# Interleaving the two parts of the up weights and shifting a row buffer by 64 bytes in a one-core decoder layer

## The chip, the cores and the metric

The kernel runs on one core of a Trainium2 chip. The core has a matrix engine (TensorE, in profiles PE, with its weight loads shown apart as PEld), a vector engine (VectorE, DVE), a scalar engine (ScalarE, ACT), a general engine (GpSimd, POOL) and a queue engine (SyncE, SP) that issues most transfers. The on-chip memory is laid out as 128 partitions; a tile has the same byte offset in all of them, and in this text an address is that offset. The metric is the time of one execution on the device in microseconds, and the kernel before takes 1039.2 us as the median of three runs (1038.97 to 1039.4).

## What is computed

One decoder layer on a sequence of 1024 rows of 1024 float32 values. A token mixer with two head groups comes first, then a gated MLP with a causal convolution of three taps:

```python
h = rms_norm(x, mix_norm)
z = h @ w_in                          # 1024 x 2320, columns for both head groups
# group A: chunked gated linear attention; group B: sliding-window attention with sinks
x = x + concat([o_gla, o_swa]) @ w_out
h2 = rms_norm(x, ffn_norm)
u = causal_dwconv(h2 @ w_up, conv_w, conv_b)      # 1024 x 5632
a, b = split(u, 2)
x = x + (silu(a) * b) @ w_down                    # 2816 -> 1024
```

The products with `w_up` (1024 x 5632) and `w_down` (2816 x 1024) are the larger part of the work.

## The kernel before, in words

**Precision.** A large product is made of float32 values that are split in two parts, a high one in the rounded type `float32r` and a low one, what is left of the value. Three matmuls replace one: high by high, high by low, low by high (`PASSES`). The function `split` makes the parts: ScalarE casts the high part into a tile (line 97), and GpSimd, or VectorE where a call says so, subtracts it from the source and writes the low part (line 100).

**Activations.** `big` holds the normalized and transposed rows of all eight row tiles, eight blocks of 128 features deep, high and low: `big[p, half, k, part, tile, column]`. `rows(t, ks, r)` is the piece of one row tile. In the first half of the program the pieces of `big` are the weights of matmuls (`dense`, line 327), and the projections' weights are the moving operand. In the MLP `big` is the moving operand: four row tiles, 512 columns, lie side by side.

**Up products.** The up projection of each block of 128 columns is done by a scheme of Strassen's kind: seven products (`P1` to `P7`) of 12 matmuls in place of eight. Each multiplies a weight operand (`A11`, `A12`, `A22` or a sum or difference `S1` to `S4`) by an activation operand. `B11`, `B21`, `B22` and `T1` lie in `big`; the sums `T2`, `T3` and `T4` lie in a second buffer, `ex`, which `norm2_sums` writes. So four of the seven products read `big` and three read `ex`. A weight operand is 4 blocks of 128 x 128, high and low, in a slot of 4096 bytes; `up_operand` (lines 782 to 808) makes it two products ahead, and `product` (line 843 issues the matmuls) uses it as the stationary side. There are 22 column blocks of each half (`a` and `b` of the MLP side by side), so 22 x 7 x 12 = 1848 up matmuls; those of the first block write banks named `gb` in the profile, all others `fb`.

**Down products.** After the third block, units of 6 down matmuls (`down_pair`, line 1024, written to `dn_P`) are put between the up products. Their operands lie in slots 4 to 7 and are written high part first, low part behind it, each in one run. VectorE adds each result to the rows `acc` (line 1028). The last two blocks go by `last_row` (line 1053).

**Order.** The order of the work is written by hand: each step gets a due time (`at`, `at_us`), the steps are sorted by it, and every engine runs its instructions in that order.

**Edges.** The convolution needs the last two values of the 512 rows before. `save_edge` (line 901) copies them out of the bank into a tile of two values; two such tiles take turns. They come from the pool `ff`, which is opened late.

**Addresses.** Pools on the left side stack upwards in the order in which they are opened: the base pool, then `acc`, then `ex`, then the pool of the second normalization, in whose place `ff` is opened afterwards. The weight slots lie on the right side. In the built program of before, `big` starts at 1152, `ex` at 112448, and the slots at addresses such as 204672. The remainder by 256 is 128 for `big` and for the slots, and 64 for `ex` and for two operands of the second block (`A11`, `A12`), which lie in the normalization's pool.

Some matmuls of the mixer are plain float32 and count twice in the profile: the scores of the linear attention (`ga`, line 601) are of this kind. The matmuls `dec` (line 548) have two columns only.

Of the kernel before, what the change touches and what calls it, by code (L numbers as in the profile page):

```python
# [9 lines left out]
F32 = mybir.dt.float32  # L10
F32R = mybir.dt.float32r
# [6 lines left out]
P = 128  # L18
T = 1024
D = 1024  # L20
NT = T // P
KD = D // P
# [12 lines left out]
def hymba_layer_kernel(ctx, tc, x, mix_norm, w_in, w_alpha2, b_alpha, gla_norm,  # L35
# [3 lines left out]
    act, dve, pool, pe, sp = nc.scalar, nc.vector, nc.gpsimd, nc.tensor, nc.sync  # L39
# [10 lines left out]
    base = ctx.enter_context(tc.tile_pool(name="base", bufs=1))  # L50
# [4 lines left out]
    def bank(name):  # L55
        ps["n"] += 1
        if "f" in ps:
            return ps["f"][2 + ps["n"] % 2]

        for start, which in (("n2pt_6", "b"), ("do1_7", "a"), ("n2pt_3", "a")):  # L60
            if name.startswith(start):
                return ps[which].tile([P, 512], F32, tag="b", name=name)
        return ps["ab"[ps["n"] % 2]].tile([P, 512], F32, tag="b", name=name)

    big = base.tile([P, 2, KD, 2, 4, P], F32R, name="big")

    def rows(t, ks, r):
        return big[:, t // 4, ks, r, t % 4, :]

    RAW_BUFS, K4, K2, N_WARM = 3, 6, 5, 5  # L70

# [13 lines left out]
    def slot_tile(slot, name, dt=F32R):  # L85
        return w_keep.tile([P, 2, 512], dt, tag=f"w{slot}", name=name, bufs=1)
# [8 lines left out]
    def split(src, hi, lo, eng=None, hi_eng=None):  # L95
        if hi_eng is None:
            act.copy(hi, src)  # L97
        else:
            hi_eng.tensor_copy(hi, src)
        (eng or pool).tensor_sub(lo, src, hi.bitcast(F32))  # L100
# [89 lines left out]
    def norm1_tr(t, i):  # L190
        tr_hi(t, i, xts["h", t], "n1")

    def norm1_lo(t, i):
        tr_lo(t, i, "n1")
# [32 lines left out]
    def norm2_sums(t):  # L227

        i, ex, pn = t - 4, fin["ex"], fin["pn"]
        p0, p1 = fin["pb", t]  # L230

        def put(src, hi, lo):
            split(src, hi, lo, dve)

        def extra(n):
            return ex[:, n, :, 0, i, :], ex[:, n, :, 1, i, :]

        def own(ks):
            return rows(t, ks, 0), rows(t, ks, 1)

        b12 = pn.tile([P, 4, P], F32, tag="b12", name=f"b12_{t}", bufs=1)
        b11, b21 = ([rows(i, ks, r).bitcast(F32) for r in range(2)] for ks in (slice(0, 4), slice(4, 8)))
        act.copy(b12, p0)
        put(p1, *own(slice(4, 8)))
        dve.tensor_sub(p0, p0, b11[0])
        dve.tensor_sub(p0, p0, b11[1])
        put(p0, *own(slice(0, 4)))
        dve.tensor_sub(p1, p1, b12)
        put(p1, *extra(1))
        dve.tensor_add(p1, p1, b11[0])  # L250
        dve.tensor_add(p1, p1, b11[1])
        put(p1, *extra(0))
        dve.tensor_sub(p0, b21[0], p1)
        dve.tensor_add(p0, p0, b21[1])
        put(p0, *extra(2))

    trs = {}

    def tr_hi(t, q, h, tag):
        pt = bank(f"{tag}pt_{t}_{q}")  # L260
        for k in range(4):
            c = (q * 4 + k) * P
            pe.transpose(pt[:, k * P:(k + 1) * P], h[:, c:c + P], ident)
        trs[tag, t, q] = pt.rearrange("p (k c) -> p k c", k=4)
        act.copy(rows(t, slice(q * 4, q * 4 + 4), 0), trs[tag, t, q])

    def tr_lo(t, q, tag):
        hi, lo = (rows(t, slice(q * 4, q * 4 + 4), r) for r in range(2))
        dve.tensor_sub(lo, trs[tag, t, q], hi.bitcast(F32))

    def norm_tr(t, h, tag):
# [5 lines left out]
    blocks = {}  # L277
# [45 lines left out]
    def dense(t, ws, n, name):  # L323
        pb = bank(name)
        for k in range(KD):
            for i, (ra, rb) in enumerate(PASSES):
                pe.matmul(pb[:, :n], lhsT=rows(t, k, ra), rhs=ws[k][:, rb, :n],  # L327
                          start=(k == 0 and i == 0), stop=(k == KD - 1 and i == 2))
        return pb

# [299 lines left out]
    def gate_tr(t, gs):  # L630
        pb = bank(f"ogt{t}")
        for h in range(4):
            pe.transpose(pb[:, h * P:(h + 1) * P], gs[:, h * P:(h + 1) * P], ident)
        pv = pb.rearrange("p (h c) -> p h c", h=4)
        hi, lo = (rows(t, slice(0, 4), r) for r in range(2))
        act.activation(hi, pv, AF.Copy, scale=glan)
        dve.scalar_tensor_tensor(lo, pv, glan, hi.bitcast(F32), op0=ALU.mult, op1=ALU.subtract)
        src = qo[:, t, :].rearrange("p (j c) -> p j c", j=4)
        hi, lo = (rows(t, slice(4, 8), r) for r in range(2))
        split(src, hi, lo)  # L640


    fin = {}
# [19 lines left out]
    def open_norm2():  # L663
        st.close()
        w_late["pool"] = swp.enter_context(tc.tile_pool(name="wb", bufs=1, side="right"))
        xp = ctx.enter_context(tc.tile_pool(name="xp", bufs=1))
        fin["ex"] = xp.tile([P, 3, 4, 2, 4, P], F32R, name="ex")
        fin["sn"] = ExitStack()
        pn = fin["pn"] = fin["sn"].enter_context(tc.tile_pool(name="pn", bufs=1))
        ffn = fin["ffn"] = pn.tile([P, D], F32, name="ffn")  # L670
        sp.dma_start(ffn, ffn_norm.partition_broadcast(P).rearrange("p o d -> p (o d)"))
        fin["s1"] = pn.tile([P, 4, P], F32, name="s1_0")
# [18 lines left out]
    psb = {}  # L691
# [18 lines left out]
    def unit_q_part(t, k0, k1):  # L710
        if k0 == 0:
            psb["q", t] = bank(f"dq{t}")
        pb = psb["q", t]
        for k in range(k0, k1):

            for i, (ra, rb) in enumerate(((0, 0), (1, 0), (0, 1))):
                pe.matmul(pb, lhsT=rows(t, k, ra), rhs=blocks["q"][k][:, rb, :],  # L717
                          start=(k == 0 and i == 0), stop=(k == KD - 1 and i == 2))

    def q_done(t):  # L720
# [56 lines left out]
    def sums(s1, a11, a21, a22, eng=pool):  # L777
        eng.tensor_add(s1, a21, a22)
        eng.tensor_sub(a21, a11, a21)
        eng.tensor_sub(a11, s1, a11)  # L780
# [7 lines left out]
    def up_operand(ch, name):  # L788
        ra, rb = raws["u", ch, 0], raws.get(("u", ch, 1), raws["u", ch, 0])
        a11, a12, a21, a22 = ra[:, 0:4], ra[:, 4:8], rb[:, 0:4], rb[:, 4:8]  # L790
        src = {"A11": a11, "A12": a12, "A21": a21, "A22": a22, "S2": a11, "S3": a21,
               "S4": a11 if ch else a12}.get(name)
        if name == "S2" and ch:
            s1 = psb["S1", ch] = fin["ff"].tile([P, 4, P], F32, tag="s", name=f"S1_{ch}", bufs=1)
            sums(s1, a11, a21, a22)
        elif name == "S1":
            src = psb["S1", ch]
        elif name == "S4" and ch:
            pool.tensor_sub(a11, a12, a11)
        slot = U_SLOT.get((ch, name))  # L800
        if slot is None:
            slot = 1 + -turn[0] % 3
            turn[0] += 1
            U_SLOT[ch, name] = slot
        w = fin["pn"].tile([P, 2, 512], F32R, name=f"{name}w_{ch}") if slot < 0 else slot_tile(slot, f"{name}w_{ch}")
        w = w.rearrange("p r (k n) -> p r k n", k=4)
        split(src, w[:, 0], w[:, 1], dve if ch < 2 and name[1] == "1" and name[0] == "A" else None)
        blocks["u", ch, name] = w

    def b_operand(name, k, r):  # L810
        ex = fin["ex"]
        return {"B11": big[:, 0, k, r], "B21": big[:, 0, 4 + k, r],
                "B22": big[:, 1, 4 + k, r], "T1": big[:, 1, k, r],
                "T2": ex[:, 0, k, r], "T3": ex[:, 1, k, r], "T4": ex[:, 2, k, r]}[name]

    PROD = {"P1": ("A11", "B11"), "P2": ("A12", "B21"), "P3": ("S4", "B22"), "P4": ("A22", "T4"),
            "P5": ("S1", "T1"), "P6": ("S2", "T2"), "P7": ("S3", "T3")}
# [77 lines left out]
        act.copy(dst, pb)  # L895

    def save_edge(ch, key, pb):
        e = psb[key, ch] = fin["ff"].tile([P, 2], F32, tag="e", name=f"{key}_{ch}", bufs=2)
        act.copy(e, pb[:, 510:512])

    def c11(ch):
# [196 lines left out]
    for c in halves:  # L1098
        split(mix_row[:, c], mix_hl[0][0:1, c], mix_hl[1][0:1, c], dve)
        pb = bank(f"mix{len(mix_ps)}")  # L1100
# [77 lines left out]
    for t in range(NT):  # L1178
        s = 11.0 + 1.9 * t
        at(s - (0.7 if t == 4 else 0.3), swa_qt, t)  # L1180
        at(s + 1.0, swa_scores, t, 0)
        at(s + 1.6, swa_scores, t, 1)
        at(s + 3.2, swa_pt, t, 0)
        at(s + 3.8, swa_pt, t, 1)
        at(s + 4.9, swa_pv, t)
        s = TG + t
        at(s - 2.4, gla_lh, t)
        at(s - 1.4, gla_exp, t)
        at(s + 1.0, gla_tr, t)
        if t < NT - 1:  # L1190
            if t:
                at(s + 1.75, gla_mid, t + 1)
            at(s + 1.8, gla_state, t)
        at(s + 1.9, gla_a, t)
        at(s + 2.7, gla_o, t)
        at(TR + t + 1.3, lambda tt=t: gate_tr(tt, psb.pop(("r", tt))))
# [23 lines left out]
    for ch, i, name in order:  # L1220
# [7 lines left out]
        if ch < 2 or (ch, i) == (2, 0):  # L1228
            n = 0
        elif ch < L - 1 or (ch, i) == (L - 1, 0):  # L1230
            n = 1
        else:
            n = 2
# [24 lines left out]
    for p in range(NPAIR):  # L1258
        for k in range(7):

            n = 7 * p + k - 2
# [51 lines left out]
```

## Time and profile before

| | |
|---|---|
| median of three runs | 1039.2 us |
| profiled execution | 1039.1 us, span 1037.4 us |
| TensorE busy | 1030.0 us (99%), 4976 matmuls |
| weight loads busy | 849.3 us (82%) |
| VectorE / ScalarE / GpSimd busy | 793.4 / 480.6 / 618.4 us |
| granted clock of TensorE | full throughout |
| idle time of TensorE before up products (`fb`) | 0.0 us |

The profile shows one execution. A group of instructions is given by line, engine, operation, output and inputs, shape and count; then follow the busy time of the group in us (overlaps counted once), the mean duration of one in ns, and the idle time of the engine before them with what ended it. Matmuls overlap: the next one starts before the last has ended, so a mean duration is longer than the distance from one to the next. That distance is read from the timeline, where equal neighbours are merged into one row with start, length and count.

### The profile page before, as it was taken

To read this page: it belongs to the slowest core of one execution; us is meant where nothing else is said; L and a number is where in the kernel's file an instruction comes from. 1 tells how busy PE (TensorE), PEld (TensorE's weight loads), DVE (VectorE), ACT (ScalarE), POOL (GpSimd) and SP (SyncE) were. 2 spreads that over 40 slices of the span, in tenths; PEclk is the share of its full clock that TensorE was granted. 3 is DMA by queue.
4 is the path that set the end of the run, shared out by engine and by line. 5 is a ranking of instruction groups with operands and counts; after the bars stand their busy time and mean duration, and the time that the engine had idled before them with its cause. 6 is when DMAs were issued, how large, how long until landed. Compare 5 with 4: busy or idle time off the path is not lost.

```text
span 1037.4 us, 13921 instructions
## 1 busy us (share of the span) xinstructions
PE 1030.0 (99%) x4976; PEld 849.3 (82%) x4976; DVE 793.4 (76%) x1332; ACT 480.6 (46%) x988; POOL 618.4 (60%) x510
## 2 busy tenths in 40 slices
PE   9999999999999999999999999999999999999998
PEld 6899887888888888888888888888888888888887
DVE  6776667755131699887979899897979798998976
ACT  5627655445340446554444445444444444454441
POOL 4592132325550205867868787877778787978750
PEclk9999999999999999999999999999999999999999
DMA  6152113002044202112120111222121211121104
GB/s 217 61 154 62 45 50 93 21 1 82 1 122 163 61 1 82 41 41 82 41 81 26 57 45 57 61 62 62 41 82 41 62 41 47 55 62 61 41 21 162
DMA packets 67502, 67.13 MB, mean 65 GB/s; under 512 B 4648, under 2 KB 52201, under 8 KB 67434
## 3 DMA queue, kind: packets, MB, share of 16 engines
q1 hardware_dynamic: 63448, 61.27, 18.9%
q10 hardware_dynamic: 3986, 4.99, 2.0%
q8 instruction: 39, 0.64, 0.2%
q14 instruction: 29, 0.24, 0.1%
HBM read 57.33 MB, written 4.19 MB: 59 GB/s over the span
## 4 chain that ended last, share of the span: by engine, by line
PE 97%; DMA 1%; DVE 1%; ACT 0%; issue 0%; POOL 0%; DVEq 0%; ACTq 0%; SPq 0%
PE fb L843 39%; PE dn_P L1024 18%; PE do L327 8%; PE dr L327 4%; PE dg L327 4%; PE dv L327 4%; PE dq L327 3%; PE dk L327 2%; PE gb L843 2%; PE dq L717 1%; PE pv L500 1%; PE fb L1053 1%; PE dl L1053 1%; PE go L610 1%; PE ga L601 1%; PE sc L453 1%
## 5 line engine op out<-in xcount | busy, mean ns | idle before, releaser
L1028 DVE TENSOR_TENSOR acc<-acc,dn_P 128x1024 f32<-128x1024 f32 x140 | 169.9, 1215 | 61.5 <-PE dn_P L1024 60.3
L1024 PE MATMUL dn_P<-dw,dg 128*128 128x512 f32 x840 | 214.0, 390 | 0.0
L1024 PEld LDWEIGHTS dn_P<-dw,dg 128*128 128x128 f32 x840 | 157.6, 188 | 34.5
L327 PE MATMUL do<-wow,big 128*128 128x512 f32 x384 | 90.9, 393 | 0.0
L100 POOL TENSOR_TENSOR dw<-dn,dw 128x512 fp32r<-128x512 f32 x50 | 68.8, 1376 | 25.3 <-ACT dw L97 24.1
L327 PEld LDWEIGHTS do<-wow,big 128*128 128x128 f32 x384 | 71.1, 188 | 14.4
L895 ACT COPY ca<-fb 128x512 f32<-128x512 f32 x62 | 36.3, 586 | 68.2 <-PE fb L843 68.2
L843 PE MATMUL fb<-ex,S2w 128*128 128x512 f32 x252 | 62.5, 394 | 0.0
L843 PE MATMUL fb<-ex,S3w 128*128 128x512 f32 x252 | 62.5, 394 | 0.0
L850 DVE SCALAR_TENSOR_TENSOR ua<-fb,cc,ua 128x511 f32<-128x511 f32 x84 | 62.2, 741 | 0.3
L843 PE MATMUL fb<-ex,A22w 128*128 128x512 f32 x252 | 62.2, 394 | 0.0
L843 PE MATMUL fb<-big,A11w 128*128 128x512 f32 x252 | 61.2, 389 | 0.0
L843 PE MATMUL fb<-big,S1w 128*128 128x512 f32 x252 | 61.1, 389 | 0.0
L843 PE MATMUL fb<-big,S4w 128*128 128x512 f32 x252 | 61.1, 389 | 0.0
L843 PE MATMUL fb<-big,A12w 128*128 128x512 f32 x252 | 60.9, 390 | 0.0
L843 PEld LDWEIGHTS fb<-ex,S2w 128*128 128x128 f32 x252 | 47.2, 187 | 11.3
L843 PEld LDWEIGHTS fb<-ex,A22w 128*128 128x128 f32 x252 | 47.2, 187 | 11.3
L843 PEld LDWEIGHTS fb<-ex,S3w 128*128 128x128 f32 x252 | 47.2, 187 | 11.3
L843 PEld LDWEIGHTS fb<-big,S1w 128*128 128x128 f32 x252 | 47.3, 188 | 10.0
L843 PEld LDWEIGHTS fb<-big,A11w 128*128 128x128 f32 x252 | 47.3, 188 | 10.0
L843 PEld LDWEIGHTS fb<-big,S4w 128*128 128x128 f32 x252 | 47.3, 188 | 10.0
L843 PEld LDWEIGHTS fb<-big,A12w 128*128 128x128 f32 x252 | 47.2, 188 | 9.8
(432 smaller groups left out, 2392.1 us busy)
## 6 DMA issues: line engine op xcount, KB each, us to landing
up<-in_w_up_dram SPq DMA_DIRECT2D x44, 512.0 KB, 3.8
dn<-in_w_down_dram SPq DMA_DIRECT2D x22, 512.0 KB, 3.5
acc<-in_x_dram SPq DMA_DIRECT2D x8, 512.0 KB, 6.5
out_dram<-acc SPq DMA_DIRECT2D x15, 256.0 KB, 2.0
xt<-in_x_dram SPq DMA_DIRECT2D x7, 512.0 KB, 3.2
vraw<-in_w_in_dram SPq DMA_DIRECT2D x4, 512.0 KB, 3.9
graw<-in_w_in_dram SPq DMA_DIRECT2D x4, 512.0 KB, 3.7
qt<-qt ACTq DMA_DIRECT2D x16, 128.0 KB, 2.2
```

The lines of the kernel that those rows point to most:

```text
L100: (eng or pool).tensor_sub(lo, src, hi.bitcast(F32))
L327: pe.matmul(pb[:, :n], lhsT=rows(t, k, ra), rhs=ws[k][:, rb, :n], start=(k == 0 and i == 0), stop=(k == KD - 1 and i == 2))
L453: pe.matmul(pbs[-1][:, j % 2, :], lhsT=ql[:, g, qc], rhs=kt[:, g, kc], start=False, stop=True)
L500: pe.matmul(pbs[i][HALF[g]], lhsT=vv[rows, t - 1 + b, HALF[g]], rhs=rhs[rows, :, HALF[i]], start=start, stop=stop)
L601: pe.matmul(pb[:, pr * 256:(pr + 1) * 256], lhsT=gqt[t][:, pr, :], rhs=qbd[t % 2][:, pr], start=(pr == 0), stop=(pr == 1))
L610: pe.matmul(pb[:, h * P:(h + 1) * P], lhsT=asb[:, h, :], rhs=v[:, h * P:(h + 1) * P], start=(h == 0), stop=(t == 0 and h == 3))
L843: pe.matmul(pb, lhsT=w[:, ra, k, :], rhs=b_operand(bn, k, rb), start=(onto is None and i == 0), stop=(i == 11), skip_group_check=onto is n ...
L850: dve.scalar_tensor_tensor(dst, src, w, dst, op0=ALU.mult, op1=ALU.add)
L895: act.copy(dst, pb)
L1024: pe.matmul(pb[:, i], lhsT=g[:, ra, c:c + P], rhs=w[:, rb, :], start=(onto is None and n == 0), stop=(n == 2), skip_group_check=onto is no ...
L1028: dve.tensor_add(acc, acc, pb)
L1053: pe.matmul(pb[:, c0:c1], lhsT=g[:, ra, (t % 4) * P:(t % 4 + 1) * P], rhs=w[:, rb, c0:c1], start=(ch == NCH - 2 and i == 0), stop=(ch == N ...
```

## The change

Three things are altered in the layout of tiles. The two parts of an up operand alternate value by value in its slot (`p (k n r) -> p r k n` in place of one part behind the other), so the weights of one matmul lie 8 bytes apart. `big` and `ex` are laid out by row tile first, so that the moving operand of an up product is four runs of 128 values, 8192 bytes apart in `big` and 4096 in `ex`; a piece of one row tile is 128 values side by side as before. The edge tiles are taken from the base pool, 64 bytes for both, which shifts what is opened after it: `ex` starts at 112512, the two operands of the second block shift too, and all operands of up products then have the remainder 128 by 256. The slots keep their addresses, and so does the convolution's pool behind the edge tiles. Helper functions that the new layout doesn't need are gone.

Both programs have the same instructions in the same order on every engine, with the same waits; only addresses and steps within operands differ.

```diff
-    big = base.tile([P, 2, KD, 2, 4, P], F32R, name="big")
-
-    def rows(t, ks, r):
-        return big[:, t // 4, ks, r, t % 4, :]
+    big = base.tile([P, NT, KD, 2, P], F32R, name="big")
...
-        act.copy(rows(t, slice(q * 4, q * 4 + 4), 0), trs[tag, t, q])
+        act.copy(big[:, t, q * 4:q * 4 + 4, 0, :], trs[tag, t, q])
...
-                pe.matmul(pb[:, :n], lhsT=rows(t, k, ra), rhs=ws[k][:, rb, :n],
+                pe.matmul(pb[:, :n], lhsT=big[:, t, k, ra, :], rhs=ws[k][:, rb, :n],
...
-        fin["ex"] = xp.tile([P, 3, 4, 2, 4, P], F32R, name="ex")
+        fin["ex"] = xp.tile([P, 3, 4, 4, 2, P], F32R, name="ex")
...
         w = fin["pn"].tile([P, 2, 512], F32R, name=f"{name}w_{ch}") if slot < 0 else slot_tile(slot, f"{name}w_{ch}")
-        w = w.rearrange("p r (k n) -> p r k n", k=4)
+        w = w.rearrange("p a c -> p (a c)").rearrange("p (k n r) -> p r k n", k=4, r=2)
         split(src, w[:, 0], w[:, 1], dve if ch < 2 and name[1] == "1" and name[0] == "A" else None)
...
-        return {"B11": big[:, 0, k, r], "B21": big[:, 0, 4 + k, r],
-                "B22": big[:, 1, 4 + k, r], "T1": big[:, 1, k, r],
-                "T2": ex[:, 0, k, r], "T3": ex[:, 1, k, r], "T4": ex[:, 2, k, r]}[name]
+        return {"B11": big[:, 0:4, k, r, :], "B21": big[:, 0:4, 4 + k, r, :],
+                "B22": big[:, 4:8, 4 + k, r, :], "T1": big[:, 4:8, k, r, :],
+                "T2": ex[:, 0, :, k, r, :], "T3": ex[:, 1, :, k, r, :],
+                "T4": ex[:, 2, :, k, r, :]}[name]
...
-        e = psb[key, ch] = fin["ff"].tile([P, 2], F32, tag="e", name=f"{key}_{ch}", bufs=2)
+        e = psb[key, ch] = base.tile([P, 2], F32, tag="e", name=f"{key}_{ch}", bufs=2)
```

More of the change, by code (lines that the diff above doesn't have):

```diff
@@ L230, in norm2_sums, with put @@
         p0, p1 = fin["pb", t]
[L232 to L239, printed above, removed]
+        def put(src, dst):
+            split(src, dst[:, :, 0, :], dst[:, :, 1, :], dve)
         b12 = pn.tile([P, 4, P], F32, tag="b12", name=f"b12_{t}", bufs=1)
-        b11, b21 = ([rows(i, ks, r).bitcast(F32) for r in range(2)] for ks in (slice(0, 4), slice(4, 8)))
+        b11, b21 = big[:, i, 0:4].bitcast(F32), big[:, i, 4:8].bitcast(F32)
         act.copy(b12, p0)
[L244 to L247, printed above, removed]
+        put(p1, big[:, t, 4:8])
+        dve.tensor_sub(p0, p0, b11[:, :, 0, :])
+        dve.tensor_sub(p0, p0, b11[:, :, 1, :])
+        put(p0, big[:, t, 0:4])
         dve.tensor_sub(p1, p1, b12)
[L249 to L255, printed above, removed]
+        put(p1, ex[:, 1, i])
+        dve.tensor_add(p1, p1, b11[:, :, 0, :])
+        dve.tensor_add(p1, p1, b11[:, :, 1, :])
+        put(p1, ex[:, 0, i])
+        dve.tensor_sub(p0, b21[:, :, 0, :], p1)
+        dve.tensor_add(p0, p0, b21[:, :, 1, :])
+        put(p0, ex[:, 2, i])
     trs = {}
@@ L264, in tr_hi @@
         trs[tag, t, q] = pt.rearrange("p (k c) -> p k c", k=4)
-        act.copy(rows(t, slice(q * 4, q * 4 + 4), 0), trs[tag, t, q])
+        act.copy(big[:, t, q * 4:q * 4 + 4, 0, :], trs[tag, t, q])
     def tr_lo(t, q, tag):
-        hi, lo = (rows(t, slice(q * 4, q * 4 + 4), r) for r in range(2))
+        hi, lo = big[:, t, q * 4:q * 4 + 4, 0, :], big[:, t, q * 4:q * 4 + 4, 1, :]
         dve.tensor_sub(lo, trs[tag, t, q], hi.bitcast(F32))
@@ L634, in gate_tr @@
         pv = pb.rearrange("p (h c) -> p h c", h=4)
-        hi, lo = (rows(t, slice(0, 4), r) for r in range(2))
+        hi, lo = big[:, t, 0:4, 0, :], big[:, t, 0:4, 1, :]
         act.activation(hi, pv, AF.Copy, scale=glan)
@@ L638, in gate_tr @@
         src = qo[:, t, :].rearrange("p (j c) -> p j c", j=4)
-        hi, lo = (rows(t, slice(4, 8), r) for r in range(2))
+        hi, lo = big[:, t, 4:8, 0, :], big[:, t, 4:8, 1, :]
         split(src, hi, lo)
@@ L716, in unit_q_part @@
             for i, (ra, rb) in enumerate(((0, 0), (1, 0), (0, 1))):
-                pe.matmul(pb, lhsT=rows(t, k, ra), rhs=blocks["q"][k][:, rb, :],
+                pe.matmul(pb, lhsT=big[:, t, k, ra, :], rhs=blocks["q"][k][:, rb, :],
                           start=(k == 0 and i == 0), stop=(k == KD - 1 and i == 2))
```

## The prediction

> **What bounds the kernel now.** I read the page first, then the waits, then groups by shape, then single stretches of the timeline. The page's first lines, its clock line and its chain of what ended last:
>
> ```profile
> span 1037.4 us, 13921 instructions
> PE 1030.0 (99%) x4976; PEld 849.3 (82%) x4976; DVE 793.4 (76%) x1332; ACT 480.6 (46%) x988; POOL 618.4 (60%) x510
> ...
> PEclk9999999999999999999999999999999999999999
> ...
> PE 97%; DMA 1%; DVE 1%; ACT 0%; issue 0%; POOL 0%; DVEq 0%; ACTq 0%; SPq 0%
> ```
>
> TensorE is busy for 1030.0 of 1037.4 us at full clock, and the chain is TensorE for 97%. The waits of TensorE, in full:
>
> ```profile
> PE warm L1094 <- DVE warm L128: 1.7, 1, 1.7
> PE dg L327 <- ACT vg L730: 1.0, 1, 1.0
> PE dq L717 <- POOL qw L305: 0.3, 1, 0.3
> PE sc L453 <- DMA ql<-ql: 0.3, 1, 0.3
> PE gb L843 <- ACT big L265: 0.2, 1, 0.2
> PE dq L717 <- DVE big L269: 0.2, 1, 0.2
> ```
>
> They add up to 3.7 us, and 0.2 us of it lies in the up products (gb). So nothing is gained by feeding TensorE earlier; a change helps only if a matmul itself takes less time. A busy TensorE need not be at its best rate, so I asked how far apart consecutive matmuls are. Groups by shape (columns: count, busy us, mean ns of one, idle before), one product on each operand, its weight load, the same kind in the first column block, and the down matmuls:
>
> ```profile
> L843 PE MATMUL fb<-ex,S2w 128*128 128x512 f32 x252 | 62.5, 394 | 0.0
> L843 PE MATMUL fb<-big,S1w 128*128 128x512 f32 x252 | 61.1, 389 | 0.0
> L843 PEld LDWEIGHTS fb<-ex,S2w 128*128 128x128 f32 x252 | 47.2, 187 | 11.3
> L843 PE MATMUL gb<-ex,S2w 128*128 128x512 f32 x12 | 3.2, 404 | 0.0
> L1024 PE MATMUL dn_P<-dw,dg 128*128 128x512 f32 x840 | 214.0, 390 | 0.0
> ```
>
> The mean duration overlaps the next matmul, so it isn't the period. The period comes from the timeline of TensorE alone (start, length of the merged group, count):
>
> ```profile
> 697.10 2.88 PE L843 MATMUL fb<-big,A12w 128*128 128x512 f32 x12
> 699.82 1.52 PE L1024 MATMUL dn_P<-dw,dg 128*128 128x512 f32 x6
> 701.18 2.96 PE L843 MATMUL fb<-ex,S2w 128*128 128x512 f32 x12
> 703.98 1.54 PE L1024 MATMUL dn_P<-dw,dg 128*128 128x512 f32 x6
> 705.36 2.88 PE L843 MATMUL fb<-big,S1w 128*128 128x512 f32 x12
> ```
>
> Twelve matmuls are eleven periods and one duration. On big: (2.88 - 0.389) / 11 = 226.5 ns. On ex: (2.96 - 0.394) / 11 = 233.3 ns. Shape, type and weight slots are alike; what differs in the built program is where the moving operand starts: big and the slots at 128 bytes over a multiple of 256, ex at 64 over. So the time of a matmul depends on how its addresses stand to those of the weights that load meanwhile. That carries on for a moment: the six matmuls of a down unit start 1.36 us before the next product when they follow big (701.18 - 699.82) and 1.38 us when they follow ex (705.36 - 703.98), though their own addresses agree.
>
> How low could the period go? The score matmuls of the linear attention (ga) show it, and the two-column matmuls (dec) show how fast weights can load:
>
> ```profile
> 201.88 1.03 PE L601 MATMUL ga<-qbd,gkt 128*128 128x256 f32 x4
> L601 PE MATMUL ga<-qbd,gkt x32: 377/379/483, 180.3 to 256.9; 128*128 128x256 f32 x32
> 209.98 0.58 PE L548 MATMUL dec<-ind,lh 128*128 128x2 f32 x4
> L548 PE MATMUL dec<-ind,lh x32: 165/250/250, 143.9 to 222.8; 128*128 128x2 f32 x32
> ```
>
> ga: (1.03 - 0.379) / 3 = 217 ns for 256 plain float32 columns, 0.85 ns a value, 4.7 bytes per ns. dec: (0.58 - 0.250) / 3 = 110 ns for a load of 128 values, 0.86 ns a value, 4.7 bytes per ns when they lie side by side. In ga the moving operand and the load therefore walk through memory at one speed, and it shows the shortest period of this size. In the up products the moving operand is read at 512 x 4 bytes in 226.5 ns, 9.0 bytes per ns, about twice the load's speed, and 9.5 ns (226.5 - 217) or 16.3 ns (233.3 - 217) are lost.
>
> My reading is that the two streams meet in a part of memory that only one can use at a time, that this repeats within 256 bytes, and that a fast stream overtaking a slow one meets it again and again. ga agrees, but it also reads at half the rate, so it is not proof.
>
> **The change, part by part.** No instruction is added, removed or moved, and no wait changes; only addresses and steps do.
>
> (a) The two 32-byte edge tiles move from a late pool into the base pool. Everything allocated after it on that side shifts by 64 bytes, so ex, and the two slots in the norm pool that the second column block uses, come to 128 over a multiple of 256. By the rows above an ex product then costs what a big one does: 233.3 - 226.5 = 6.8 ns. There are 22 blocks x 3 products x 12 = 792 such matmuls (3 groups of x252, 3 of x12): 5.4 us. There are 840 / 6 = 140 down units, and 3 of 7 products read ex, so some 60 of them follow ex and gain 1.38 - 1.36 = 0.02 us each: 1.2 us. Together 6.6 us, which is the surest term.
>
> (b) Up weights: high and low parts alternate, so a load of 128 values steps 8 bytes and spans 1024 bytes. If it keeps its 0.86 ns a value it walks at 9.3 bytes per ns, the moving operand's speed. By my reading a stream that yields once is then behind the other and stays there: the losses of 9.5 and 16.3 ns go, down to the 217 ns of ga. Big: 22 x 4 x 12 = 1056 matmuls x 9.5 = 10.0 us. Ex: 792 x 16.3 = 12.9 us, which contains the 5.4 us of (a). With the 1.2 us: 24.1 us. Against it stands the change of pattern between up and down, since a down unit after an up product with other steps may have to settle as it does behind ex now: 0 to 140 x 0.02 = 2.8 us; I take the middle, 1.4. No row has a load with such steps. The bounds are the 217 ns of ga below and, if every load costs by the memory it spans, 217 + 2 x 9.5 = 236 ns above; I take the lower, since ga is the one row whose two streams keep pace.
>
> (c) The moving operand of an up product becomes four runs of 128 values, 8192 or 4096 bytes apart, where it was one run of 512. A run is 512 bytes and the hops are multiples of 256, so the place within 256 bytes goes on as before. No four-run row of this type exists; the bounds are nothing and, if each of three hops cost one value (226.5 / 512 = 0.44 ns), 1.3 ns x 1848 = 2.4 us. I take nothing, keep the other end for the range.
>
> (d) Writers. ScalarE's cast now writes every second word, and GpSimd's subtraction reads and writes so. Their present price, the load of one stretch the length of a pair of column blocks, and one operand's way to its product:
>
> ```profile
> L100 POOL TENSOR_TENSOR S3w<-up,S3w 128x512 fp32r<-128x512 f32 x22 | 33.0, 1501 | 20.2 <-ACT S3w L97 20.2
> L97 ACT CAST S4w<-up 128x512 fp32r<-128x512 f32 x22 | 13.8, 627 | 0.0
> 740.00:798.00 58.00, 58.00 (x255) 47.49 (x254) 51.20 (x64) 27.45 (x47) 45.51 (x34) 1.00 0.18 55
> 700.76 1.29 POOL L100 TENSOR_TENSOR S3w<-up,S3w 128x512 fp32r<-128x512 f32 x1 [1.93 <-ACT S3w L97]
> 709.44 2.73 PE L843 MATMUL fb<-ex,S3w 128*128 128x512 f32 x11
> ```
>
> In the windows row the columns after PE and its weight loads are VectorE 51.20, ScalarE 27.45, GpSimd 45.51 of 58 us. I cost it at nothing: S3w is ready at 702.05 and used at 709.44, 7.4 us of cover, and fourteen subtractions in a pair may grow by (58 - 2.2 - 45.5) / 14 = 0.7 us each, half their price, before GpSimd fills the shortened pair (24 us over 11 pairs is 2.2 us). ScalarE has over 2 us for each of its casts. VectorE, at 51.2 of 55.8, keeps 4.6 us. [...]
>
> **Sum.** Profiled span 1037.4 - 24.1 + 1.4 = 1014.7; the profiled execution took 1039.1, so 1.7 us lie around the span: 1016.4, I say 1016. The profiled execution stands 0.1 us under the median of 1039.2, so it needs no correction.
>
> **The rivals.**
>
> Alignment alone: the interleaving neither helps nor hurts, because plain float32 in ga is quick for its half rate and not for its equal speed. Then (a) remains: 1039.1 - 6.6 = 1032.5. For it: the 233.3 against 226.5 ns is measured, the equal-speed idea isn't.
>
> Nothing: the loads never take from the running matmul and the 6.8 ns have another cause. 1039. [...]
>
> Slower, more memory per load: each load now spans 1024 bytes instead of 512, and if the loss goes with the memory touched it doubles to 19 ns. Period 236 ns: 1056 x 9.5 + 792 x (236 - 233.3) - 1.2 = 11.0 us more, 1050. It decides as soon as the loss grows with the span at all instead of falling. [...] Against: at one and the same span it differs, 9.5 and 16.3 ns, so places count, not bytes alone.
>
> [...]
>
> **How the numbers follow.** Both streams at one speed: 0.57, time 1016, own range 1012 (217 ns is good to 1 ns, 1.8 us, and no settling) to 1024 (half of the 9.5 ns stays, 8.8 us, with the hops of (c)). Alignment alone: 0.18. Nothing: 0.05. Memory per load: 0.13. Single words: 0.07. I leave out the last two, 0.20, so the range is 1012 to 1040. About 0.2% is what this measurement tells from no change. Faster 0.57 + 0.18 = 0.75, same 0.05, slower 0.20.
>
> **What would show it.** Right for (a): ex and big products have one period, and down units behind ex last 1.36 us. Right for (b): twelve up matmuls merge to 11 x 0.217 + 0.38 = 2.77 us, while down units keep 1.52. Settling: a 1.54 there. (d): casts near 0.62 and subtractions near 1.3 to 1.5 us, no new row of TensorE waiting for GpSimd. Wrong: 2.88 throughout (alignment alone), near 2.98 (memory per load), or weight loads longer than the matmuls.

## The result, and the profile after

The changed kernel took 1044.95 us (median; 1044.81 to 1045.64) against 1039.28 us for the kernel before on the same chip: a ratio of 1.0056, interval 1.0039 to 1.0074. It became slower, by 5.7 us, where 23 us less were forecast.

The page after, its first lines and its chain of what ended last:

```profile
span 1043.9 us, 13921 instructions
PE 1036.7 (99%) x4976; PEld 859.8 (82%) x4976; DVE 796.8 (76%) x1332; ACT 486.3 (47%) x988; POOL 621.0 (59%) x510
...
PE 97%; DVE 1%; DMA 1%; ACT 0%; issue 0%; POOL 0%; DVEq 0%; ACTq 0%; SPq 0%
```

The span grew by 6.5 us (1043.9 - 1037.4) and TensorE's busy time by 6.7 (1036.7 - 1030.0), at the same full clock. The loss lies inside the matmuls: TensorE is still the chain, and its waits are the same few:

```profile
PE warm L1086 <- DVE warm L125: 1.7, 1, 1.7
PE dg L318 <- ACT vg L721: 1.1, 1, 1.1
```

The groups by shape after (count, busy us, mean ns of one, idle before): up products on each operand, their weight loads, the down matmuls, and the two writers of S3w.

```profile
L835 PE MATMUL fb<-ex,S2w 128*128 128x512 f32 x252 | 62.5, 394 | 0.0
L835 PE MATMUL fb<-big,S1w 128*128 128x512 f32 x252 | 62.7, 394 | 0.0
L835 PEld LDWEIGHTS fb<-big,S1w 128*128 128x128 f32 x252 | 48.7, 193 | 10.0
L1016 PE MATMUL dn_P<-dw,dg 128*128 128x512 f32 x840 | 213.8, 390 | 0.0
L97 POOL TENSOR_TENSOR S3w<-up,S3w 128x512 fp32r<-128x512 f32 x22 | 33.3, 1512 | 21.3 <-ACT S3w L94 21.3
L94 ACT CAST S3w<-up 128x512 fp32r<-128x512 f32 x22 | 14.5, 658 | 47.4 <-issue 24.5 <-PE fb L835 19.8 <-POOL S1w L97 3.1
```

Matmuls on ex have kept their 62.5 us; those on big have gone from 61.1 to 62.7. The loads take 193 ns where they took 187 (for products on ex) or 188 (on big): single words aren't slow to load. The timeline of TensorE after (start, length, count) says the same by single products:

```profile
700.39 2.96 PE L835 MATMUL fb<-big,A12w 128*128 128x512 f32 x12
703.19 1.53 PE L1016 MATMUL dn_P<-dw,dg 128*128 128x512 f32 x6
704.56 2.96 PE L835 MATMUL fb<-ex,S2w 128*128 128x512 f32 x12
707.36 1.53 PE L1016 MATMUL dn_P<-dw,dg 128*128 128x512 f32 x6
```

All up products now have the period of ex before, (2.96 - 0.394) / 11 = 233.3 ns. Ex and big have become equal, as forecast, but at the bad value: big lost the 6.8 ns that the shift was to take off ex (233.3 - 226.5). A down unit starts 1.37 us before the next product behind either operand (704.56 - 703.19), between the 1.36 and 1.38 of before.

Summed over the whole trace, for each matmul the distance from the start of the one before it to its own start, in us (the four columns on the right belong to the experiments below):

| | before | after | shift alone | interleaving alone | shift + interleaving | shift + runs |
|---|---|---|---|---|---|---|
| up on big, 1056 | 240.0 | 246.4 | 240.2 | 246.4 | 246.4 | 239.9 |
| up on ex, 792 | 184.6 | 184.7 | 179.8 | 182.5 | 184.7 | 179.9 |
| down, 840 | 191.9 | 191.8 | 190.6 | 192.7 | 191.8 | 190.6 |
| all others, 2287 | 415.4 | 415.6 | 416.1 | 416.0 | 415.6 | 415.2 |
| sum | 1032.0 | 1038.5 | 1026.7 | 1037.6 | 1038.5 | 1025.6 |

From before to after the sum rises by 6.5 us, and 6.4 of it lies in the up products on big.

### The profile page after: what moved, and what is told of

Read it like the earlier page. It is cut to its first block, busy times and chain, and to the rows that moved or that the text cites. A ratio compares the mean times of both kernels' runs of the same rounds, so it can differ in the third digit from the quotient of the medians.

```text
span 1043.9 us, 13921 instructions
## 1 busy us (share of the span) xinstructions
PE 1036.7 (99%) x4976; PEld 859.8 (82%) x4976; DVE 796.8 (76%) x1332; ACT 486.3 (47%) x988; POOL 621.0 (59%) x510
## 4 chain that ended last, share of the span: by engine, by line
PE 97%; DVE 1%; DMA 1%; ACT 0%; issue 0%; POOL 0%; DVEq 0%; ACTq 0%; SPq 0%
PE fb L835 39%; PE dn_P L1016 18%; PE do L318 8%; PE dr L318 4%; PE dv L318 4%; PE dg L318 4%; PE dq L318 3%; PE dk L318 2%; PE gb L835 2%; PE dq L708 1%; PE pv L491 1%; PE dl L1045 1%; PE fb L1045 1%; PE go L601 1%; PE ga L592 1%; PE sc L444 1%
## 5 line engine op out<-in xcount | busy, mean ns | idle before, releaser
L1020 DVE TENSOR_TENSOR acc<-acc,dn_P 128x1024 f32<-128x1024 f32 x140 | 169.8, 1214 | 63.1 <-PE dn_P L1016 62.7
L835 PE MATMUL fb<-big,S1w 128*128 128x512 f32 x252 | 62.7, 394 | 0.0
L835 PE MATMUL fb<-big,S4w 128*128 128x512 f32 x252 | 62.7, 394 | 0.0
L835 PE MATMUL fb<-ex,S3w 128*128 128x512 f32 x252 | 62.5, 394 | 0.0
L835 PE MATMUL fb<-ex,S2w 128*128 128x512 f32 x252 | 62.5, 394 | 0.0
```

The lines of the kernel that those rows point to most:

```text
L835: pe.matmul(pb, lhsT=w[:, ra, k, :], rhs=b_operand(bn, k, rb), start=(onto is None and i == 0), stop=(i == 11), skip_group_check=onto is n ...
L1020: dve.tensor_add(acc, acc, pb)
```

## The experiments

**The parts, one by one.** The change has three parts that can act on TensorE: the shift of 64 bytes, the interleaved weights, the moving operand in four runs. Theory A in the expectations: interleaving itself costs, and hides a gain of the shift. B: the four runs cost. C: the shift is worth nothing. Four kernels tell them apart.

Shift alone: the kernel before, with only the edge tiles moved.

```
-        e = psb[key, ch] = fin["ff"].tile([P, 2], F32, tag="e", name=f"{key}_{ch}", bufs=2)
+        e = psb[key, ch] = base.tile([P, 2], F32, tag="e", name=f"{key}_{ch}", bufs=2)
```

> The kernel before with the edge tiles in the base pool and nothing else, so ex comes to the remainder 128 of the slots. Theory A (the 8-byte steps of the weight loads cost the running matmul, and the shift itself is a gain): ex products fall from 233.3 to 226.5 ns like big ones, twelve of them merge to 2.88 us, down units behind ex from 1.38 to 1.36 us; 1039.2 - 6.6 = 1032.6 us. Theory B (the four runs of the moving operand cost 6.8 ns, the steps of the loads nothing): the same here, 1032.6. Theory C (the 233 ns belong to ex whatever its address, and the shift is worth nothing or harms): 1039 us.

It took 1033.29 us (1032.74 to 1033.89) against 1039.63 for the kernel before in the same session: a ratio of 0.9940 (0.9928 to 0.9953), 6.3 us less (5.3 us in the table, which is of one execution). The timeline of TensorE of this kernel:

```profile
699.03 2.88 PE L843 MATMUL fb<-ex,S2w 128*128 128x512 f32 x12
701.75 1.52 PE L1024 MATMUL dn_P<-dw,dg 128*128 128x512 f32 x6
703.11 2.88 PE L843 MATMUL fb<-big,S1w 128*128 128x512 f32 x12
705.83 1.52 PE L1024 MATMUL dn_P<-dw,dg 128*128 128x512 f32 x6
707.19 2.88 PE L843 MATMUL fb<-ex,S3w 128*128 128x512 f32 x12
```

The product on ex has become as short as that on big, 2.88 us, and the down unit behind ex starts 1.36 us ahead of the next product (703.11 - 701.75), as that behind big does (707.19 - 705.83). C falls.

Interleaving alone: the kernel before, with only the weights' layout changed.

```
-        w = w.rearrange("p r (k n) -> p r k n", k=4)
+        w = w.rearrange("p a c -> p (a c)").rearrange("p (k n r) -> p r k n", k=4, r=2)
```

> The kernel before with up weights interleaved and nothing else: moving operands stay one run, ex stays 64 bytes off. Theory A (steps of the loads cost): big products go from 226.5 to about 233, ex products change in a way that no row told so far, between 226.5 and 240; with ex unchanged 1039.2 + 1056 x 6.8 = 1046.4 us. Theory B (the four runs cost): nothing changes, 1039.2 us, loads may last 193 ns all the same. Theory C (the shift harms): 1039 us.

It took 1044.37 us (1043.57 to 1045.37), a ratio of 1.0047 (1.0034 to 1.0060). Its timeline:

```profile
700.10 2.96 PE L843 MATMUL fb<-big,A12w 128*128 128x512 f32 x12
702.90 1.53 PE L1024 MATMUL dn_P<-dw,dg 128*128 128x512 f32 x6
704.27 2.92 PE L843 MATMUL fb<-ex,S2w 128*128 128x512 f32 x12
707.03 1.55 PE L1024 MATMUL dn_P<-dw,dg 128*128 128x512 f32 x6
```

This line alone takes the products on big from 2.88 to 2.96 us. Those on ex, whose moving operand still has the remainder 64, get 2.92 instead of 2.96: the places of the two streams still count, but they count otherwise.

Both edits together, with the moving operand left in one run:

> Shift and interleaving, but the moving operands in one run as before. Theory A: like the changed kernel, all up matmuls at 233.3 ns, 1044.9 us. Theory B: without the four runs big and ex products are at 226.5 ns or below, 1032.6 us or less.

It took 1045.75 us (1045.27 to 1046.76), a ratio of 1.0062 (1.0049 to 1.0075). Its timeline:

```profile
700.43 2.96 PE L843 MATMUL fb<-big,A12w 128*128 128x512 f32 x12
704.59 2.96 PE L843 MATMUL fb<-ex,S2w 128*128 128x512 f32 x12
```

Ex and big are both at 2.96 us, as in the changed kernel, without its four runs. On top of interleaving the shift gains nothing: ex goes from 182.5 to 184.7 us in the table, down units from 192.7 to 191.8, and the two intervals overlap. Without interleaving it gained 6.3 us. The edits don't add up.

The changed kernel with only the interleaving taken back, so that shift and four runs remain:

```
-        w = w.rearrange("p a c -> p (a c)").rearrange("p (k n r) -> p r k n", k=4, r=2)
+        w = w.rearrange("p r (k n) -> p r k n", k=4)
```

> The changed kernel without the interleaving: shift and four runs of the moving operand, weights of an operand high part first and low part behind. Theory A: all up matmuls at 226.5 ns, 1032.6 us, the fastest together with the kernel that has the shift alone. Theory B: all at 233.3 ns, 1044.9 us.

It took 1033.44 us (1032.76 to 1033.89), a ratio of 0.9942 (0.9929 to 0.9956), the same as the shift alone. Its timeline:

```profile
701.98 2.88 PE L835 MATMUL fb<-big,S1w 128*128 128x512 f32 x12
706.06 2.88 PE L835 MATMUL fb<-ex,S3w 128*128 128x512 f32 x12
```

The four runs cost nothing: B falls. A holds: interleaving costs 12.5 us over the shift (1045.75 - 1033.29), and it is the only part that costs. Shift alone and shift with runs beat both kernels.

**Is it the place of the two streams?** The next kernel leaves the layer out and runs bare matmuls, 20 of a kind on constant data, so its time is not comparable with the layer's. The weights stay in place, and the moving operand's start is varied. Its cases are named by the step of the weights (plain: one stretch; alt: every second value; four, eight: every fourth, every eighth) and by a letter for the start (a: 0, e: 64, i: 128, m: 192, p: 240 bytes over that of the weights, modulo 256).

> A kernel that leaves the layer out and only writes x to the output; it issues groups of 20 matmuls of the up products' shape, all in one tile, to measure the period by itself. 'plain' loads 128 values side by side and moves the start of the moving operand by 16 bytes a case, 0 to 496; 'alt' loads every second value over 0 to 240 bytes, 'altlow' from the odd word; 'four', 'eight', 'thirtytwo' and 'sixtyfour' load every 4th, 8th, 32nd and 64th value; 'runs' has four runs of the moving operand; 'movalt' and 'bothalt' step the moving operand, or both, by two values. Theory P (two streams meet in places that repeat within 256 bytes): plain has 226.7 ns at 0 and 233.3 at 192 bytes more (64 less), the same pattern again from 256 on; alt has some offsets near 217 ns and others well above 233, so the changed kernel only stands at a bad one. Theory Q (each line of memory that a load touches costs the running matmul, places matter little): alt is 233 ns or more at every offset, four higher still, eight and above the same as four. runs equals plain under both.

This kernel and the two after it ran once each, at full clock. The timeline of TensorE of the bare matmuls:

```profile
24.99 4.70 PE L51 MATMUL plain_aa<-buf 128*128 128x512 f32 x20
80.67 4.82 PE L51 MATMUL plain_am<-buf 128*128 128x512 f32 x20
99.21 4.73 PE L51 MATMUL plain_aq<-buf 128*128 128x512 f32 x20
173.48 4.82 PE L51 MATMUL alt_aa<-buf 128*128 128x512 f32 x20
229.34 4.77 PE L51 MATMUL alt_am<-buf 128*128 128x512 f32 x20
275.98 4.94 PE L51 MATMUL four_ai<-buf 128*128 128x512 f32 x20
361.12 9.18 PE L51 MATMUL movalt_aa<-buf 128*128 128x512 f32 x20
```

and the groups for the durations of some, with the loads:

```profile
L51 PE MATMUL plain_aa<-buf 128*128 128x512 f32 x20 | 4.7, 389 | 0.0
L51 PEld LDWEIGHTS plain_aa<-buf 128*128 128x128 f32 x20 | 3.8, 188 | 0.8
L51 PEld LDWEIGHTS alt_aa<-buf 128*128 128x128 f32 x20 | 3.9, 193 | 0.8
L51 PEld LDWEIGHTS four_ai<-buf 128*128 128x128 f32 x20 | 4.9, 310 | 0.0
L51 PE MATMUL movalt_aa<-buf 128*128 128x512 f32 x20 | 9.2, 631 | 0.0
```

Twenty matmuls are nineteen periods and one duration: (4.70 - 0.389) / 19 = 226.9 ns for plain_aa. The first matmuls of a case still settle, as plain_aq shows (4.73, the case 256 bytes on), so the table takes the last eleven distances between single starts, in ns:

| start over the weights', bytes mod 256 | 0 | 64 | 128 | 192 | 240 |
|---|---|---|---|---|---|
| weights in one stretch | 226.7 | 228.8 | 233.0 | 233.5 | 226.7 |
| weights every second value | 233.4 | 233.5 | 231.6 | 230.0 | 233.6 |

Starts were tried in steps of 16 bytes. With plain weights the cases from 256 bytes on give the same periods as those from 0 on, within 0.1 ns, so the pattern repeats at 256 bytes. The four cells in columns 0 and 192 are the kernels: operands that agree, plain, 226.7 (big before, shift alone); ex before at 64 against 128, which is 192, plain, 233.5 (233.1 in its trace); interleaved at 0, 233.4 (changed kernel); interleaved at 192, 230.0 (ex in interleaving alone, 230.4). The bare matmuls give these periods without the layer's writers, waits and order. With every second value no one of the 16 starts gets under 230.0. So theory P is right that places count (plain loads range from 226.7 to 235.0 ns) and wrong that a start near 217 ns can be found; theory Q is wrong that places matter little. Four runs of the moving operand gave 226.7, 229.2, 231.8 and 233.5 ns at the starts 0, 64, 128 and 192, within 1.2 ns of one run.

Here only the moving operand is shifted, so its own place could be what counts. The kernel before has the other case: the weights of the second block, `A11` and `A12`, lie at 64, and the moving operand in `big` keeps its 128, which is the start 64. The last six distances within that `A12` product (from 403.7 us on) are 229, 232, 226, 229, 232 and 225 ns, 228.8 in the mean, the table's value for 64; with the shift alone, where both are at 128, they are 226 and 227. So the place of one against the other counts.

**Why then was ga at 217 ns?** A second kernel of bare matmuls (the layer left out again) takes ga's kind, 256 columns of plain float32, with loads in one stretch (fpplain) and with every second value (fpalt). It also loads fewer values (third: 32), or one word 128 times (oneword).

> A second kernel that leaves the layer out and only writes x to the output, with groups of 20 matmuls in one tile. 'fine' moves the start of the moving operand by 4 bytes a case from 32 bytes before the weights' place to 28 behind it, plain loads; 'third', 'half', 'most' load 32, 64, 96 values instead of 128; 'oneword' loads the same word 128 times; 'fpplain' and 'fpalt' are plain float32 with 256 columns, weights side by side or every second; 'short' and 'mid' have 256 and 384 columns. Theory Q (what a load touches costs the running matmul): third, half and most lose a quarter, a half and three quarters of what 128 values lose (9.5 ns at 0, 16.3 ns at 192 bytes), oneword loses next to nothing, about 217 ns, and fpalt is as fast as fpplain only if plain float32 is free because it reads at half the rate. Theory R (equal speed is what makes plain float32 free): fpplain 216 ns at every offset, and fpalt, whose load is twice as fast through memory as the moving operand, loses 7 to 16 ns. Theory S (the loss has nothing to do with loads): third and oneword keep 226.7 and 233 ns.

Its timeline, in which a plain float32 matmul counts twice:

```profile
99.85 4.79 PE L52 MATMUL third_aa<-buf 128*32 128x512 f32 x20
155.26 4.80 PE L52 MATMUL oneword_aa<-buf 128*128 128x512 f32 x20
173.80 8.79 PE L52 MATMUL fpplain_aa<-buf 128*128 128x256 f32 x40
208.33 8.80 PE L52 MATMUL fpalt_aa<-buf 128*128 128x256 f32 x40
```

and the groups for the durations:

```profile
L52 PE MATMUL fpalt_aa<-buf 128*128 128x256 f32 x40 | 8.8, 379 | 0.0
L52 PE MATMUL fpplain_aa<-buf 128*128 128x256 f32 x40 | 8.8, 379 | 0.0
L52 PE MATMUL third_aa<-buf 128*32 128x512 f32 x20 | 4.8, 394 | 0.0
L52 PEld LDWEIGHTS third_aa<-buf 128*32 128x32 f32 x20 | 2.2, 109 | 2.4
```

Plain float32 has (8.79 - 0.379) / 39 = 215.7 ns with loads in one stretch, where both streams walk at one speed, and (8.80 - 0.379) / 39 = 215.9 with every second value, where they don't. All four starts of each gave 215.8 or 215.9. The equal speed wasn't the reason: theory R falls. And a load of 32 values, a quarter of the memory, leaves (4.79 - 0.394) / 19 = 231.4 ns at start 0, where a load of 128 has 226.7, so the loss doesn't go by the amount loaded either, and theory Q falls; 64 and 96 values gave 228.0 to 233.5 ns over four starts. One word loaded 128 times leaves (4.80 - 0.394) / 19 = 231.9 ns, or 231.5 by the last eleven distances, at each of four places of the moving operand. Changing only the load moves the period, so theory S, that loads have no part in it, falls too. The loads of 32, 64, 96 and 128 values took 109, 134, 161 and 188 ns, (188 - 109) / 96 = 0.82 ns a value, and 193 ns with every second value: by these durations the interleaved loads did walk about twice as fast. In steps of 4 bytes around 0, plain loads gave 226.7 at -20, -16, -4, 0 and 28, and up to 240.1 (at -12). Narrower float32r products lose otherwise: with 256 columns 120.0 and 113.4 ns at the starts 0 and 192 with plain loads, so that 0 is the slower one, and 120.0 and 120.2 with every second value, with 384 columns 173.3 or 173.4 in all four cases.

A third kernel of bare matmuls, without the layer, asks whether the moving operand's rate decides: operands of two bytes a value (sixteen, sixteenalt), and a moving operand that reads one word 512 times and so walks nowhere (movword, movwordalt).

> A third kernel that leaves the layer out and only writes x to the output, with groups of 20 matmuls. 'altfine': every-second loads with the start of the moving operand moved by 4 bytes a case, from 32 before to 28 behind. 'sixteen' and 'sixteenalt': 16-bit operands, loads plain and every second. 'movword' and 'movpair': the moving operand reads one word, or one pair of words, over and over; the 'alt' forms with every-second loads. 'width' and 'widthalt': 508, 504, 500, 496, 480, 448 columns. Theory R2 (a moving operand of 4 bytes a column at full rate has no spare turn, so 226.7 ns is its best and 217 was never to be had): sixteen has about 216 ns at every offset and with either load; altfine has no offset under 226.7 ns. Theory P (the loads' places decide, and a right place gives 217 ns): some altfine offset is near 217 ns, and movword or movpair, which stay in one place, fall to 217 ns as well. Theory G (the period comes in fixed steps of 6.67 ns): width keeps steps, 496 columns 6.67 ns under 512 and 508 to 500 at the one or the other.

Its timeline:

```profile
24.28 4.80 PE L57 MATMUL altfine_aa<-buf 128*128 128x512 f32 x20
99.09 4.49 PE L57 MATMUL sixteen_aa<-half 128*128 128x512 bf16 x20
116.37 4.48 PE L57 MATMUL sixteenalt_aa<-half 128*128 128x512 bf16 x20
129.32 4.48 PE L57 MATMUL sixteenalt_am<-half 128*128 128x512 bf16 x20
133.44 4.72 PE L57 MATMUL movword_aa<-buf 128*128 128x512 f32 x20
138.00 4.54 PE L57 MATMUL movwordalt_aa<-buf 128*128 128x512 f32 x20
```

Sixteen-bit operands, half the bytes per ns, give 215.8 ns with either kind of load at every start tried. A moving operand that stays in place gives (4.54 - 0.381) / 19 = 218.9 ns even with loads of every second value (218.7 by the last eleven starts). That speaks against theory R2 as it stands, which ties the loss to four bytes a column at full rate; its forecasts for sixteen-bit operands and for the 16 starts below hold. Narrowing the product to 480 and 448 columns brought both kinds of load to about one period (216.6 and 216.9, 203.0 and 203.5 ns); 496 columns with plain loads took 223.3 ns, not the 220.0 of theory G. With loads in one stretch, movword has a longer row, 4.72 us, but its first matmul starts 0.2 us before twenty sixteen-bit periods are over (133.44 against 129.32 + 20 x 0.2158 = 133.64); from there to the next row it has (138.00 - 133.64) / 20 = 218 ns. At 512 columns, periods of 226.7 ns and more appear in these runs only where a float32r moving operand walks, and how long they are depends on how its places meet those of the load (226.7 to 240.1 ns for loads of 128 values in one stretch). Sixteen more starts with every second value, 4 bytes apart (altfine), gave 232.2 to 236.0 ns: none of the starts tried for that layout is as good as 0 is for weights in one stretch.

No run shows that the two streams meet in a part of memory that only one can use at a time; that was the reading of the prediction. What stays open is the law by which places meet: why loads of every second value never reach 226.7 ns, and why the best case of 512 walking float32r values stays 11 ns over sixteen-bit operands. Matmuls without any load between them weren't tried.

## Why the prediction was wrong, and where it was right

**What bounds the kernel** was right: TensorE alone, and only the period of a matmul counts. Waits and order didn't change.

**(a), the shift,** was right in place and size: 6.6 us forecast, 6.3 measured when it stands alone. By the table, whose sums differ by 5.3 us, 4.8 lie on ex (5.4 forecast) and 1.3 on the down units (1.2 forecast), and the other matmuls take 0.7 more. In the changed kernel the gain can't be seen, because interleaving sets another price for the same addresses.

**(b), the interleaving, is the step that failed:** "I take the lower, since ga is the one row whose two streams keep pace". The lower was 217 ns; measured were 233.3 on both operands, near the other bound of 236. The text itself had said that ga "also reads at half the rate, so it is not proof", and the doubt was justified: in ga's kind the period is 215.8 ns whether the streams keep pace or not. That half the rate is what makes it short fits the sixteen-bit operands, but ga also differs in type, and no run separates the two. So the reading that a stream which yields once stays behind falls: the loads kept their pace, 193 ns for 188, and two streams at about one speed met as badly as ex and its weights did before. In us: 10.0 on big were to be gained, 6.4 were lost; 12.9 on ex were to be gained, 0.1 was lost. The 1.4 us for settling were near the 1.2 us by which down units rise from shift alone to shift with interleaving (190.6 to 191.8), by luck, since 1.4 was only the middle of 0 to 2.8.

**(c), four runs,** was right at nothing: 2.88 us with them and without.

**(d), the writers,** was right in that they stay hidden. The cast of S4w went from 627 to 663 ns, that of S3w from 621 to 658, and the subtraction of S3w from 1501 to 1512, and no wait on them appeared.

**A sum in the range.** The upper end of its own range for (b), 1024, doesn't follow from the terms named for it: 1016.4 + 8.8 + 2.4 = 1027.6. The stated range, 1012 to 1040, doesn't rest on it.

**The rivals.** The alignment rival was right that ga isn't quick for its equal speed, and gave interleaving a price of nothing; it cost 12.5 us. Memory per load came nearest in time, 1050, with 236 ns where 233.3 came, but by luck: its mechanism falls with the 32-value loads at 231.4 ns. What the runs show in its place is that loads of every second value have periods of their own by start, 230.0 to 236.0 ns, and that the changed kernel's start, 0, has 233.4, where most of them lie; no rival had that. The 0.07 for single words has no run behind it: no run shows loads of every second word that are slow enough to set the period. They took 193 ns where loads in one stretch took 187 or 188, and the period beside them was 233.3. A moving operand that takes every second word did take longer: movalt_aa has (9.18 - 0.631) / 19 = 450 ns, about twice 226.7.

**Loads and the running matmul.** The shift alone changes nothing but places and gains 6.3 us. That the loads never take from the running matmul, as the rival "nothing" had it, isn't borne out for float32r of 512 columns, where the load's layout alone moves the period (226.7, 231.5 and 233.4 ns at start 0 for one stretch, one word and every second value). The sixteen-bit rows (215.8 ns with either kind of load) and the plain float32 rows (215.8 or 215.9 ns) agree with that rival.

## What to carry to other kernels

Where two things differ between the row that you have and the row that you hope for, a price can't be taken from it: ga differed in rate, in type and in equal speed, and the equal speed didn't matter, so the alignment alone, which had a row on both sides, was the forecast to make. For float32r products of 512 columns, start the moving operand at the same remainder by 256 bytes as the weights that load meanwhile, and keep those in one stretch (226.7 ns here, against 233.5 at 192 bytes more and 233.4 with every second value); then look at the length of twelve merged matmuls, 2.88 or 2.96 us here. Try such layout edits one at a time, since the best start of one layout (0 for weights in one stretch) isn't that of another (192 for every second value, 230.0 ns), nor of another width (at 256 columns with weights in one stretch, 192 has 113.4 ns and 0 has 120.0).

## What was not expected of the hardware

A load may take longer than the distance from one matmul to the next without setting it. Loads of every fourth value took 310 ns (four_ai) and the period was (4.94 - 0.401) / 19 = 238.9 ns (401 ns is the mean duration of those matmuls): consecutive loads overlap. A price that lets the load's length set the period would have been far too high here, 310 ns for 238.9.

Steps of 32 and of 64 values, which take a load over 16 and 32 KB, gave 233.3 to 234.5 and 233.3 to 240.0 ns, no worse than steps of four (235.4 to 239.9), while steps of eight were the worst (244.5 to 246.6). The span of a load doesn't order them.
